# The first layer's gate and up projections as seven half products per pair of output tiles, with the down projection in a stage of its own

## The chip, the cores and the metric

The kernel runs on one core of one Trainium2 chip. The metric is the device time of one execution in microseconds (us), taken as the median of three runs.

## The reference, cut to what matters

The reference is one inference step of a two-layer decoder trunk for 1024 prompt tokens and 64 sample tokens (1088 together), with a model width of 1024. Layer 0 mixes tokens with a short gated convolution, layer 1 with a Conformer convolution. After the mixer, each layer adds a feed-forward part and a gated embedding:

```python
h = h + mix
h = h + swiglu_ffn(rms_norm(h, g_ffn[i]), ffn_w_gu[i], ffn_w_down[i])
gate = jax.nn.sigmoid(rms_norm(h, g_ple[i]) @ ple_w_gate[i])
h = h + gate * (p[i] @ ple_w_proj[i])

def swiglu_ffn(x, w_gu, w_down):
    g, u = jnp.split(x @ w_gu, 2, axis=-1)
    return (jax.nn.silu(g) * u) @ w_down
```

The hidden width of the feed-forward part is 2816, so `x @ w_gu` is 1088 x 1024 by 1024 x 5632, and the down projection is 1088 x 2816 by 2816 x 1024. Everything is float32.

## The kernel before

Activations lie transposed, with 128 channels on the partitions and tokens along the free axis: `h[0]` to `h[7]` are the eight tiles of the residual stream, 128 x 1088 each. A float32 product is made of three matmuls in a faster format: weights and data are each split into a high part and a low part (the rest), and `block` (L259) adds high x high, high x low and low x high. All tokens of layer 0 form the group `GJ`, whose 1088 columns are three matmuls of 288, 512 and 288 columns.

`item` (L274) makes one output tile: for each tile of the contraction a block of 9 matmuls, into one of two PSUM buffers of the pool `ps_j`. Weights come in units of 128 x 1024 (eight blocks). `prep_to` (L201) keeps three units ready: a DMA on SyncE's queue into one of two raw buffers, a ScalarE copy to `whi`, and for `wlo` a GpSimd subtraction `raw - whi`. For later layers, whose units are used twice, `stage` (L231) works ahead during the first layer's feed-forward part: every 6.3 us of a modelled TensorE clock it loads a unit on ScalarE's DMA queue, copies it to the one buffer `shi` on ScalarE, subtracts on GpSimd, and writes the low part to DRAM (`dlo`); later, `wlo` is loaded from there. There are 110 such units.

Instructions are written out by hand in program order, and each engine works through its own in that order. SyncE and ScalarE each issue their DMAs in order, too, and wait before a DMA whose data or buffer isn't ready.

Layer 0 runs as `mixer_a` (L448) and `ffn` (L516), both through `hidden` (L496), which mixes up projections with partial down projections over a few hidden tiles (`MIX_SPLIT`, `FFN_SPLIT`). After an `item` of a down projection VectorE adds it to `h` (`add_h`, L440). In the last part of a down projection, each finished tile of `h` is split at once for the next stage (`norm_split`: ScalarE writes the high part, VectorE the low part), and its squares are added up (`norm_stat`, L377: ScalarE squares, GpSimd or VectorE adds). The sum over channels and its reciprocal root `r` (`rms`, L422) are made while the next stage already multiplies; `r` is applied to the products:

```python
for f in up:    psg = item(y); t = silu(psg * r) * r; psu = item(y); t = psu * t; split t into act
for j in 0..7:  h[j] += item(act tiles of this part)
```

In the code, each hidden tile of the feed-forward part (22 of them) is thus two items of eight blocks.

Of the kernel before, what the change touches and what calls it, by code (L numbers as in the profile page):

```python
# [13 lines left out]
F32 = mybir.dt.float32  # L14
F32R = mybir.dt.float32r
# [45 lines left out]
MIX_SPLIT = [2, 3, 3]  # L61
N_UNITS_0 = 4 * KD + 3 * KF
# [17 lines left out]

GB1 = Group(HALF, 320, [(0, 320)], 0, 512)
# [56 lines left out]
class Net:  # L138
# [3 lines left out]
    def __init__(self, ctx, tc, xT, wall, pT, sa, sb, vecs, yT, sa_p, sa_s, sb_p, sb_s):  # L142
# [11 lines left out]
        self.to_stage = deque(dict.fromkeys(self.order[len(first):]))  # L154
        self.staged, self.staging, self.stage_raw = {}, None, deque()
        self.pst, self.stage_at = None, 0.0
# [9 lines left out]

    def fetch_to(self, n):
        while self.n_raw < min(n, len(self.order)):
            i = self.n_raw % (self.RAW + len(self.spare))
            if i < self.RAW:  # L170
                t = self.pw.tile([P, KD * P], F32, name="wraw", tag="wraw", bufs=self.RAW)
# [7 lines left out]
    def fetch_first(self, piece):  # L179

        for u in range(2):
            if piece == 0:
                self.raw[u] = self.pw.tile([P, KD * P], F32, name="wraw", tag="wraw", bufs=self.RAW)
# [4 lines left out]
    def prep_first(self, piece):  # L188
        nc = self.nc
        for u in range(2):  # L190
            if piece == 0:
                self.hi[u], self.lo[u] = (
                    self.pw.tile([P, KD * P], F32R, name=n, tag=n, bufs=self.RING)
                    for n in ("whi", "wlo"))
# [6 lines left out]
    def prep_to(self, n):  # L201

        nc = self.nc
        while self.n_prep < min(n, len(self.order)):
# [5 lines left out]
            if kind == "w":  # L210
                hi, lo = (
                    self.pw.tile([P, KD * P], F32R, name=n, tag=n, bufs=self.RING)
                    for n in ("whi", "wlo"))
# [17 lines left out]
    def stage(self):  # L231
# [4 lines left out]
        if nc.tensor.at < self.stage_at or self.pst is None:  # L236
            return
        self.stage_at = max(self.stage_at + self.STAGE_EVERY, nc.tensor.at - 2 * self.STAGE_EVERY)
        done, self.staging = self.staging, None
        nc.scalar.wait(nc.tensor)  # L240
        if done is not None:
            u, lo = done
            self.staged[u] = self.pd.tile([P, KD * P], F32, name=f"dlo{u}")
            nc.scalar.dma_start(self.staged[u], lo)
        ready = len(self.stage_raw) == self.STAGE_AHEAD or not self.to_stage
        if ready and self.stage_raw:
            u, raw = self.stage_raw.popleft()
            hi = self.pst.tile([P, KD * P], F32R, name="shi", tag="shi", bufs=1)
# [4 lines left out]
        if self.to_stage:  # L253
            u = self.to_stage.popleft()
            raw = self.pst.tile([P, KD * P], F32, name="sraw", tag="sraw", bufs=self.STAGE_AHEAD + 3)
            nc.scalar.dma_start(raw, self.wall[u])
            self.stage_raw.append((u, raw))


    def block(self, g, ps, blk, x, first, last):  # L260
# [3 lines left out]
        for i, (w, part) in enumerate(((whi, 0), (whi, 1), (wlo, 0))):  # L264
            for c, n in g.chunks:
                self.nc.tensor.matmul(
                    ps[:, g.base + c:g.base + c + n], w, x[:, part, c:c + n],
# [144 lines left out]
    def sum_p(self, g, parts, use):  # L412

        for i, (c, n) in enumerate(g.chunks):
            if g is GJ:
# [6 lines left out]
    def rms(self, g, begin, end):  # L422
# [6 lines left out]
        def two():  # L429
            v = self.tmp(g, "nv")  # L430
# [17 lines left out]
    def mixer_a(self, y):  # L448
# [44 lines left out]

        return self.hidden(g, MIX_SPLIT, up, acts, 0, "g_ffn")

    def hidden(self, g, split, up, acts, layer, gain, bg=None, swap=lambda: None, groups=None):  # L496
        groups = groups or [g]
        out = {q: [] for q in groups}
        for op in hidden_order(split):
# [4 lines left out]
            for j in range(KD):  # L504
                self.add_h(g, j, self.item(g, [acts[k0 + i] for i in range(n)]))
                if b == len(split) - 1:
                    if j == 0:
                        swap()
                    for q in groups:
                        out[q].append(self.norm_split(q, j, self.vec(gain, layer * KD + j)))  # L510
                    self.norm_stat(g, j)
                self.after(bg)
        return [out[q] for q in groups]


    def ffn(self, g, layer, y, bg=None, **kw):  # L516
# [27 lines left out]
        return self.hidden(g, FFN_SPLIT, up, acts, layer, "g_ple", bg, **kw)  # L544
# [335 lines left out]
    def run(self):  # L880
# [20 lines left out]
        for j in range(KD):  # L901
            self.h[j] = ph.tile([P, T], F32, name=f"h{j}")
# [280 lines left out]
```

## Time and profile before

| | |
|---|---|
| median of three runs | 2551.38 us (2550.46 to 2551.61) |
| profiled execution, its own time | 2547.9 us |
| its span, first to last instruction | 2546.1 us |
| mean granted TensorE clock | 0.996 |
| TensorE (PE) busy | 2518.0 us, 99% |
| VectorE (DVE), ScalarE (ACT), GpSimd (POOL) busy | 1068.5, 909.6, 978.0 us |
| DMA | 429.07 MB, mean 169 GB/s |

The times are of one execution each; the profile is of an execution of its own, which took 2547.9 us. "PE" is matmul time, "PEld" are the weight loads, which overlap it. The mixer of layer 0 runs from about 9 to 395 us of the span, its feed-forward part to about 1185 us; the rest of the kernel is the same before and after.

### The profile page before, as it was taken

What the parts mean: (1) busy time and instruction counts of PE and PEld (TensorE: products, weight loads), DVE (VectorE), ACT (ScalarE), POOL (GpSimd) and SP (SyncE); (2) the same over time, 40 slices, a digit from 0 to 9 for tenths busy, and PEclk for the clock granted to TensorE, in tenths of its full rate; (3) what the DMA queues carried; (4) which work ended last, traced back from release to release, by engine and by line L of the source; (5) the groups of instructions that cost most, each with busy time, mean ns of one, the idle gap of its engine ahead of it and who ended that gap; (6) DMA issues with size and microseconds to landing.
All of it is one profiled execution on the core that took longest, in us unless ns stands there. A gap on an engine that the chain in (4) does not pass through costs nothing.

```text
span 2546.1 us, 36304 instructions
## 1 busy us (share of the span) xinstructions
PE 2518.0 (99%) x15062; PEld 2283.9 (90%) x15062; DVE 1068.5 (42%) x1546; ACT 909.6 (36%) x1106; POOL 978.0 (38%) x552
## 2 busy tenths in 40 slices
PE   9999999999999999999999999999999999999997
PEld 8999998999999999998789897888887999999997
DVE  6222234212221212215587676787774622222235
ACT  5111123322332332325555436443435532222235
POOL 3323246756666666653244243333341210000012
PEclk9999999999999999999999999999999999999999
DMA  3111113656565656643565565555556665445445
GB/s 133 56 47 43 43 51 125 225 180 210 202 210 190 207 190 209 212 169 138 181 210 180 167 177 189 189 187 187 190 173 207 208 244 198 166 164 165 163 163 195
DMA packets 143236, 429.07 MB, mean 169 GB/s; under 512 B 33888, under 2 KB 37344, under 8 KB 143072
## 3 DMA queue, kind: packets, MB, share of 16 engines
q1 hardware_dynamic: 110240, 309.17, 36.9%
q10 hardware_dynamic: 32832, 117.59, 13.3%
q8 instruction: 118, 1.93, 0.3%
q14 instruction: 46, 0.38, 0.0%
HBM read 358.94 MB, written 67.76 MB: 168 GB/s over the span
## 4 chain that ended last, share of the span: by engine, by line
PE 96%; DVE 2%; ACT 1%; DMA 0%; issue 0%; DVEq 0%; SPq 0%; ACTq 0%
PE ps L121 96%; DVE t L121 0%; DVE nt L121 0%; DMA wlo<-dlo 0%; DVE acc L121 0%; DVE h L121 0%; DVE hna L121 0%; DVE nv L121 0%; DVE act L121 0%; DMA h<-xT 0%; ACT ua L121 0%; ACT act L121 0%; ACT L121 0%; ACT cact L121 0%; DVE r L121 0%
## 5 line engine op out<-in xcount | busy, mean ns | idle before, releaser
L121 PE MATMUL ps<-hn,whi 128*128 128x288 f32 (+3 forms) x6528 | 1322.8, 325 | 3.5 <-DVE t L121 1.7
L121 PEld LDWEIGHTS ps<-hn,whi 128*128 128x128 f32 x6528 | 1012.8, 189 | 89.7 <-issue 3.0
L121 PE MATMUL ps<-hn,wlo 128*128 128x288 f32 (+3 forms) x3264 | 795.7, 325 | 2.6 <-DMA wlo<-dlo 2.6
L121 PEld LDWEIGHTS ps<-hn,wlo 128*128 128x128 f32 x3264 | 524.9, 189 | 44.8 <-DMA wlo<-dlo 2.8
L121 PE MATMUL ps<-act,whi 128*128 128x288 f32 (+1 forms) x2496 | 511.8, 329 | 1.5 <-DVE act L121 1.4
L121 ACT ACTIVATE whi<-wraw 128x1024 fp32r<-128x1024 f32 (+1 forms) x326 | 339.3, 1043 | 345.3 <-PE ps L121 304.3
L121 PEld LDWEIGHTS ps<-act,whi 128*128 128x128 f32 x2496 | 387.4, 188 | 39.8 <-DVE act L121 2.6
L121 POOL TENSOR_TENSOR t<-t,r 128x1088 f32<-128x1088 f32 (+2 forms) x74 | 136.5, 1844 | 626.8 <-ACT t L121 581.8
L121 POOL TENSOR_TENSOR wlo<-wraw,whi 128x1024 fp32r<-128x1024 f32 (+1 forms) x98 | 240.6, 2457 | 249.7 <-ACT whi L121 233.4
L121 DVE TENSOR_TENSOR h<-ps,h 128x1088 f32<-128x1088 f32 (+2 forms) x216 | 205.5, 952 | 251.0 <-PE ps L121 250.7
L121 PE MATMUL ps<-act,wlo 128*128 128x288 f32 (+1 forms) x1248 | 303.3, 328 | 0.0
L121 POOL TENSOR_TENSOR sraw<-sraw,shi 128x1024 fp32r<-128x1024 f32 x110 | 265.7, 2415 | 79.9 <-issue 61.3
L121 DVE TENSOR_TENSOR t<-ps,r 128x512 f32<-128x512 f32 (+4 forms) x138 | 107.3, 780 | 369.9 <-PE ps L121 369.2
L121 DVE TENSOR_TENSOR t<-ps,t 128x1088 f32<-128x1088 f32 (+2 forms) x89 | 80.8, 908 | 422.5 <-PE ps L121 410.7
L121 POOL TENSOR_TENSOR sqacc<-sqacc,sq 128x512 f32<-128x512 f32 (+4 forms) x76 | 118.0, 1552 | 274.8 <-ACT sq L121 274.5
L121 PEld LDWEIGHTS ps<-act,wlo 128*128 128x128 f32 x1248 | 198.5, 188 | 18.2
L121 ACT ACTIVATE shi<-sraw 128x1024 fp32r<-128x1024 f32 x110 | 115.7, 1052 | 242.8 <-POOL sraw L121 242.0
L121 ACT ACTIVATE t<-t 128x512 f32<-128x512 f32 (+4 forms) x106 | 75.9, 717 | 334.4 <-DVE t L121 334.3
L121 POOL TENSOR_TENSOR prod<-prod 128x512 f32<-128x512 f32 x96 | 124.3, 1302 | 182.3 <-ACT prod L121 182.1
L121 ACT ACTIVATE act<-t 128x1088 fp32r<-128x1088 f32 (+2 forms) x74 | 62.4, 844 | 292.6 <-DVE t L121 292.1
L121 DVE SCALAR_TENSOR_TENSOR acc<-ub,vecs_sb,acc 128x512 f32<-128x512 f32 x184 | 137.5, 748 | 4.0 <-ACT acc L121 4.0
L121 DVE SCALAR_TENSOR_TENSOR acc<-ua,vecs_sb,acc 128x512 f32<-128x512 f32 x184 | 129.2, 750 | 6.3 <-ACT acc L121 4.8
(123 smaller groups left out, 1630.5 us busy)
## 6 DMA issues: line engine op xcount, KB each, us to landing
wraw<-wall SPq DMA_DIRECT2D x322, 512.0 KB, 3.4
wlo<-dlo SPq DMA_DIRECT2D x226, 512.0 KB, 3.4
sraw<-wall ACTq DMA_DIRECT2D x110, 512.0 KB, 4.1
dlo<-sraw ACTq DMA_DIRECT2D x110, 512.0 KB, 2.9
h<-xT SPq DMA_DIRECT2D x8, 544.0 KB, 6.4
pp<-t SPq DMA_DIRECT2D x8, 288.0 KB, 2.4
ub<-pp SPq DMA_DIRECT2D x8, 288.0 KB, 4.7
pp<-t SPq DMA_DIRECT2D x8, 256.0 KB, 2.7
```

The costliest lines, as they stand in the source:

```text
L121: return f(out, *args, **kw)
```

## The change

The gate tile and the up tile of one hidden tile `f` are taken together as the two output halves of a 2 x 2 block product: weights `A11`, `A12` (gate, lower and upper half of the contraction) and `A21`, `A22` (up), tokens in two halves of 544 (`TH`), `B11`, `B12`, `B21`, `B22`. Strassen's scheme in Winograd's form needs seven products of half size in place of eight, with sums of weights (`S1` to `S4`) and of tokens (`T1` to `T4`). One `product` has four contraction tiles, three matmul passes and two pieces of 272 columns (`GS`): 24 matmuls. Seven go into one hidden tile.

The token side (`operands`) is made in the last part of the mixer's down projection, after each second tile of `h` (order `MIX_J`, parts now 2, 2 and 4 hidden tiles); its 28 cells take the place of the old `hn` tiles and of six tiles of `h`, which is written to DRAM (`hd`). The weight side (`pair_fetch`, `pair_sums`, `pair_cell`) is made one hidden tile ahead. The hidden tiles' results go to DRAM (`ad`). Then `h` is loaded again, and `ffn0_down` makes the down projection in parts of 3, 4, 4, 4, 4 and 3 hidden tiles, each loaded and split anew. `stage` now works in half units (220) from 50 us on, every 4.4 us of the modelled clock, with a pause between the mixer's last part and the up stage; what is left is staged in `swap`, after the first item of the last part. The layer's arithmetic is otherwise the same.

```diff
-MIX_SPLIT = [2, 3, 3]
+MIX_SPLIT = [2, 2, 4]
+MIX_J = [0, 4, 1, 5, 2, 6, 3, 7]
+DOWN_0 = [3, 4, 4, 4, 4, 3]
+GS = Group(0, T, [(0, TH // 2), (TH // 2, TH // 2)], HALF - TH // 2, 1024)
...
+    def stage(self, flush=False):
+        nc = self.nc
+        if self.stage_slots is None or not flush and nc.tensor.at < self.stage_at:
             return
         self.stage_at = max(self.stage_at + self.STAGE_EVERY, nc.tensor.at - 2 * self.STAGE_EVERY)
         done, self.staging = self.staging, None
+        ahead = len(self.stage_slots) - 3
         if done is not None:
+            nc.scalar.dma_start(self.staged[u][:, i * WH:(i + 1) * WH], lo)
+        ready = len(self.stage_raw) == ahead or flush or not self.to_stage
         if ready and self.stage_raw:
             u, raw = self.stage_raw.popleft()
+            hi = self.stage_slots[0]("shi", F32R)
             nc.scalar.activation(hi, raw, AF.Copy)
             nc.gpsimd.tensor_tensor(raw.bitcast(F32R), raw, hi.bitcast(F32), ALU.subtract)
             self.staging = u, raw
+        if self.to_stage and not flush:
+            nc.scalar.dma_start(raw, self.wall[u][:, i * WH:(i + 1) * WH])
+    def stage_with(self, slots):
+        while self.stage_raw or self.staging:
+            self.stage(True)
+        self.stage_slots, self.stage_at = slots, self.nc.tensor.at
...
+    ORDER = "A11", "S2", "S3", "S1", "S4", "A12", "A22"
+    ORDER_0 = "A11", "A12", "S2", "S3", "S1", "S4", "A22"
+    def pair_fetch(self, i):
+        raw = [self.wtile("wraw", k) for k in range(2)]
+        ...
+        for k, t in enumerate(raw):
+            self.nc.sync.dma_start(t, self.wall[N_MIX + 2 * i + k])
+    def pair_sums(self, i):
+        for d, a, b, op in ("S1", "A21", "A22", ALU.add), ("S2", "S1", "A11", ALU.subtract), (
+                "S4", "A12", "S2", ALU.subtract), ("S3", "A11", "A21", ALU.subtract):
+            nc.vector.tensor_tensor(p[d], p[a], p[b], op)
+    def pair_cell(self, i, name):
+        nc.scalar.activation(w[:, 0], src, AF.Copy)
+        (nc.gpsimd if name[0] == "A" else nc.vector).tensor_tensor(
+            w[:, 1], src, w[:, 0].bitcast(F32), ALU.subtract)
+    def product(self, ps, w, xs):
+        for k, x in enumerate(xs):
+            for i, (h, part) in enumerate(((0, 0), (0, 1), (1, 0))):
+                for c, n in GS.chunks:
+                    self.nc.tensor.matmul(...)
+            self.stage()
...
+    def mixer_end(self, i, ps):
+        g, j = GJ, MIX_J[i]
+        if i == 0:
+            self.at_end[0]()
+        if i == KD - 1:
+            self.at_end[1]()
+        self.add_h(g, j, ps)
+        self.nc.sync.dma_start(self.hd[j], self.h[j])
+        if i % 2:
+            self.operands(j - KH)
+        self.norm_stat(g, j, self.nc.vector)
+        if i == KD - 3:
+            self.pair_fetch(0)
+    def operands(self, k):
+        def put(name, src, scale=None):
+            x = self.right[name, k] = pool.tile([P, 2, TH], F32R, name="y7", tag=tag, bufs=1)
+            self.split(x, src, scale)
+        put("B11", ha[:, lo], ga)
+        nc.scalar.activation(ya, ha, AF.Copy, scale=ga)
+        put("B21", hb[:, lo], gb)
+        nc.scalar.activation(yb, hb, AF.Copy, scale=gb)
+        nc.vector.tensor_tensor(ya[:, lo], ya[:, up], ya[:, lo], ALU.subtract)
+        nc.vector.tensor_tensor(ya[:, up], yb[:, up], ya[:, up], ALU.subtract)
+        put("T1", ya[:, lo])
+        nc.vector.tensor_tensor(yb[:, up], yb[:, up], ya[:, lo], ALU.subtract)
+        put("T2", yb[:, up])
+        put("B22", hb[:, up], gb)
+        put("T3", ya[:, up])
+        nc.vector.tensor_tensor(yb[:, lo], yb[:, lo], yb[:, up], ALU.subtract)
+        put("T4", yb[:, lo])
...
+    def ffn0_up(self):
+        for f in range(KF):
+            if f == 0:
+                rms[0]()
+                self.pair_fetch(1)
+            def go(a, b):
+                ps = self.psum(GS)
+                self.product(ps, self.cell.pop((f, a)), [self.right[b, k] for k in range(KH)])
+                return ps[:, GS.base:GS.base + TH]
+            nc.scalar.activation(t[:, lo], go("A11", "B11"), AF.Copy)
+            if f == 0:
+                nc.scalar.activation(t[:, up], t[:, lo], AF.Copy)
+                add(t[:, lo], go("A12", "B21"), t[:, lo])
+            next_weights(0)
+            add(t[:, up], go("S2", "T2"), t[:, lo] if f else t[:, up])
+            if f == 0:
+                rms[1]()
+            next_weights(1)
+            add(s[:, lo], go("S3", "T3"), t[:, up])
+            next_weights(2)
+            q = go("S1", "T1")
+            add(t[:, up], q, t[:, up])
+            add(s[:, up], q, s[:, lo])
+            next_weights(3)
+            add(t[:, up], go("S4", "B22"), t[:, up])
+            next_weights(4)
+            if f:
+                add(t[:, lo], go("A12", "B21"), t[:, lo])
+            nc.vector.tensor_tensor(t, t, r, ALU.mult)
+            nc.scalar.activation(t, t, AF.Silu)
+            nc.vector.tensor_tensor(s[:, up], s[:, up], r[:, up], ALU.mult)
+            add(s[:, lo], go("A22", "T4"), s[:, lo])
+            nc.vector.tensor_tensor(s[:, lo], s[:, lo], r[:, lo], ALU.mult)
+            nc.vector.tensor_tensor(t, t, s, ALU.mult)
+            nc.sync.dma_start(self.ad[f], t)
+    def ffn0_down(self, places, swap):
+        def load():
+            nc.sync.dma_start(t, self.ad[f])
+            nc.scalar.activation(high, t, AF.Copy)
+            nc.vector.tensor_tensor(low, t, high.bitcast(F32), ALU.subtract)
+        for _ in range(DOWN_0[0]):
+            load()
+        for b, n in enumerate(DOWN_0):
+            last = b == len(DOWN_0) - 1
+            for j in range(KD):
+                self.add_h(g, j, self.item(g, acts[at:at + n]))
+                if not last:
+                    if j < DOWN_0[b + 1]:
+                        load()
+                    continue
+                if j == 0:
+                    swap()
+                for q in out:
+                    out[q].append(self.norm_split(q, j, self.vec("g_ple", j)))
+                self.norm_stat(g, j)
...
+        self.pps = pool("ps_s", c_ps, space=PSUM, bufs=4)
+        self.ffn0_up()
+        self.stage_with(None)
+        self.pps = pool("ps_d", c_ps, space=PSUM, bufs=2)
+        for j in 3, 7, 4, 0, 1, 5, 2, 6:
+            nc.sync.dma_start(self.h[j], self.hd[j])
         def swap():
+            for _ in range(len(self.to_stage)):
+                self.stage_at = 0.0
+                self.stage()
+            self.stage_with(None)
+        ya, yb = self.ffn0_down(places, swap)
...
-    STAGE_EVERY = 6.3
+    STAGE_EVERY = 4.4
+    STAGE_FROM = 50.0
```

`next_weights(m)` makes the next hidden tile's `pair_sums` at m = 0 and its seven `pair_cell` at m = 1 to 4, then fetches the pair after it (for f = 0, two steps later).

## Rows read from the trace of the kernel before

**Rows 1.** The page: engines busy; below, shares of the chain of waits.

```profile
PE 2518.0 (99%) x15062; PEld 2283.9 (90%) x15062; DVE 1068.5 (42%) x1546; ACT 909.6 (36%) x1106; POOL 978.0 (38%) x552
...
PE 96%; DVE 2%; ACT 1%; DMA 0%; issue 0%; DVEq 0%; SPq 0%; ACTq 0%
```

**Rows 2.** Busy time by stretch (us, instructions), then granted clock, DMA share, GB/s.

```profile
100.00:400.00 300.00, 299.61 (x1801) 272.10 (x1801) 85.14 (x80) 62.35 (x64) 105.54 (x54) 1.00 0.16 47
400.00:420.00 20.00, 19.91 (x121) 17.86 (x120) 9.40 (x7) 5.07 (x5) 12.48 (x5) 1.00 0.43 150
420.00:800.00 380.00, 378.28 (x2287) 345.01 (x2286) 86.50 (x67) 114.76 (x112) 240.79 (x100) 1.00 0.58 198
800.00:1200.00 400.00, 399.52 (x2391) 362.94 (x2390) 98.30 (x86) 132.60 (x136) 241.45 (x100) 1.00 0.55 189
```

**Rows 3.** Timeline of the mixer: start, duration; first and last of 11 blocks.

```profile
300.16 0.95 PEld L121 LDWEIGHTS ps<-hn,whi 128*128 128x128 f32 x6
...
315.07 0.95 PEld L121 LDWEIGHTS ps<-hn,whi 128*128 128x128 f32 x6
```

**Rows 4.** Timeline, 288-column matmuls: first and last of 9 such pieces.

```profile
2451.95 0.70 PE L121 MATMUL ps<-hn,whi 128*128 128x288 f32 x4
...
2458.34 0.69 PE L121 MATMUL ps<-hn,whi 128*128 128x288 f32 x4
```

**Rows 5.** Timeline, 256-column matmuls: first and last of 15 such pieces.

```profile
2509.91 0.40 PE L121 MATMUL ps<-hn,whi 128*128 128x256 f32 x2
...
2514.90 0.40 PE L121 MATMUL ps<-hn,whi 128*128 128x256 f32 x2
```

**Rows 6.** Groups by shape: count, busy, mean ns of one, idle before, releasers.

```profile
L121 ACT ACTIVATE whi<-wraw 128x1024 fp32r<-128x1024 f32 x322 | 336.9, 1048 | 345.3 <-PE ps L121 304.3 <-issue 34.1 <-POOL sqacc L121 3.6
...
L121 POOL TENSOR_TENSOR wlo<-wraw,whi 128x1024 fp32r<-128x1024 f32 x96 | 236.6, 2465 | 239.2 <-ACT whi L121 222.9 <-issue 16.1
...
L121 ACT ACTIVATE shi<-sraw 128x1024 fp32r<-128x1024 f32 x110 | 115.7, 1052 | 242.8 <-POOL sraw L121 242.0 <-ACT whi L121 0.9
L121 DVE TENSOR_TENSOR h<-ps,h 128x1088 f32<-128x1088 f32 x88 | 113.6, 1291 | 181.1 <-PE ps L121 181.1
...
L121 DVE SCALAR_TENSOR_TENSOR hn<-h,vecs_sb,hn 128x576 fp32r<-128x576 f32 x31 | 25.3, 819 | 16.6 <-ACT hn L121 16.6
L121 ACT ACTIVATE hn<-h,vecs_sb 128x576 fp32r<-128x576 f32 x32 | 24.5, 771 | 33.8 <-DVE h L121 33.6
...
L121 ACT ACTIVATE sq<-h 128x1088 f32<-128x1088 f32 x21 | 22.8, 1097 | 0.0
...
L121 POOL TENSOR_TENSOR prod<-prod,c 128x512 f32<-128x512 f32 x14 | 18.1, 1293 | 0.1
...
L121 DVE TENSOR_TENSOR act<-t,act 128x512 fp32r<-128x512 f32 x22 | 16.0, 728 | 15.4 <-ACT act L121 15.4
...
L121 DVE SCALAR_TENSOR_TENSOR hn<-h,vecs_sb,hn 128x512 fp32r<-128x512 f32 x16 | 12.0, 752 | 12.7 <-ACT hn L121 12.7
L121 ACT ACTIVATE hn<-h,vecs_sb 128x512 fp32r<-128x512 f32 x16 | 11.6, 724 | 25.3 <-DVE h L121 25.3
```

**Rows 7.** Timeline: GpSimd and VectorE side by side.

```profile
415.66 2.56 POOL L121 TENSOR_TENSOR sraw<-sraw,shi 128x1024 fp32r<-128x1024 f32 x1 [1.99 <-ACT shi L121]
...
415.99 3.37 DVE L121 SCALAR_TENSOR_TENSOR nt<-nt,nv 128x1088 f32<-128x1088 f32 x1
```

**Rows 8.** Busy time by stretch: around a TensorE wait.

```profile
1438.00:1442.00 4.00, 1.74 (x14) 1.50 (x12) 3.56 (x7) 3.09 (x5) 2.91 (x3) 1.00 0.80 175
1442.00:1446.00 4.00, 3.69 (x19) 3.69 (x20) 2.35 (x4) 1.06 (x1) 0.50 (x1) 0.67 1.09 374
```

**Rows 9.** DMA issues: KB each, median us to landing.

```profile
wraw<-wall SPq DMA_DIRECT2D x322, 512.0 KB, 3.4
...
h<-xT SPq DMA_DIRECT2D x8, 544.0 KB, 6.4
```

**Rows 10.** Busy time by stretch: transfers at their densest.

```profile
2500.00:2510.00 10.00, 10.00 (x73) 10.00 (x72) 4.39 (x10) 5.12 (x9) 2.55 (x3) 1.00 1.01 384
```

More of the change, by code (lines that the diff above doesn't have):

```diff
@@ L153, in __init__ @@
         self.n_raw = self.n_prep = self.blk = 0
-        self.to_stage = deque(dict.fromkeys(self.order[len(first):]))
+        self.limit = N_MIX
+        self.n_conv = 0
+        self.pairs, self.cell = {}, {}
+        self.to_stage = deque((u, i) for u in dict.fromkeys(self.order[len(first):]) for i in range(2))
         self.staged, self.staging, self.stage_raw = {}, None, deque()
-        self.pst, self.stage_at = None, 0.0
+        self.stage_slots, self.stage_at = None, 0.0
         self.bg = deque()
@@ L191, in prep_first @@
             if piece == 0:
-                self.hi[u], self.lo[u] = (
-                    self.pw.tile([P, KD * P], F32R, name=n, tag=n, bufs=self.RING)
-                    for n in ("whi", "wlo"))
+                self.hi[u], self.lo[u] = self.wpair()
             c = self.FIRST[piece]
@@ L210, in prep_to @@
             if kind == "w":
-                hi, lo = (
-                    self.pw.tile([P, KD * P], F32R, name=n, tag=n, bufs=self.RING)
-                    for n in ("whi", "wlo"))
+                hi, lo = self.wpair()
             else:
@@ L503, in hidden @@
             _, b, k0, n = op
-            for j in range(KD):
-                self.add_h(g, j, self.item(g, [acts[k0 + i] for i in range(n)]))
+            for i, j in enumerate(js):
+                ps = self.item(g, [acts[k0 + i] for i in range(n)])
+                if last and b == len(split) - 1:
+                    last(i, ps)
+                    continue
+                self.add_h(g, j, ps)
                 if b == len(split) - 1:
[L507 to L510, printed above, removed]
+                    out.append(self.norm_split(g, j, self.vec(gain, layer * KD + j)))
@@ new lines, in run @@
+        self.pps = pool("ps_s", c_ps, space=PSUM, bufs=4)
+        self.PSW = GS.width
+        self.stage_with(self.stage_tiles(pool("stage_u", c_st), 5))
+        self.ffn0_up()
+        self.stage_with(None)
+        c_st.close()
+        self.n_conv += 2
+        c_x.close()
+        c_ps.close()
+        c_ps = ExitStack()
+        self.pps = pool("ps_d", c_ps, space=PSUM, bufs=2)
+        self.PSW = 0
+        py, py2 = self.cells["T2", 0][0], self.cells["B11", 0][0]
+        for j in range(KD):
+            self.h[j] = ph.tile([P, T], F32, name=f"h{j}", tag=f"h{j}")
```

198 lines of the change are left out of this document (151 added, 47 removed).

## The prediction

> **What bounds the kernel now.** I read the page first: TensorE is busy 99% of the span, and the chain of waits lies on it for 96% [rows 1]. So only two things count: how long TensorE's own work takes, and how long it is made to wait. The windows over the part that is rewritten show how little it waits today: between 100 and 1200 us it is idle for 0.39 + 0.09 + 1.72 + 0.48 = 2.7 us, at full clock, while VectorE is busy for about a quarter of the time [rows 2]. A change that shortens TensorE's work therefore gives its full saving, less every wait that it brings. The groups by shape give prices for the other engines [rows 6].
>
> **What the seven products save.** Before, a hidden tile is 16 blocks of 9 matmuls. Ten blocks start 315.07 - 300.16 = 14.91 us apart [rows 3], so one takes 1.491 us and a hidden tile 23.86. Matmuls of 272 columns aren't in the trace. Those of 288 start every (2458.34 - 2451.95) / 48 = 133.1 ns [rows 4], those of 256 every (2514.90 - 2509.91) / 42 = 118.8 ns [rows 5]; 272 lies halfway, 126.0 ns. A product is 24 of them, 3.02 us, seven are 21.2 us. The saving is 2.70 us a hidden tile, **59.4 us** over 22, about an eighth less a little for the shorter pieces. The down projection keeps its blocks, so it costs the same. The 2.7 us of old waits go, too, since each stood at an edge that no longer exists. Everything else is about new waits, and I find three.
>
> **First seam: mixer to up stage.** Each item of the mixer's last part is now four blocks, 5.96 us; a pair of items gives TensorE 11.9 us. Per pair VectorE adds twice to `h` (1.29 each), adds squares twice (like the add, 1.29) and makes the operands: seven low parts and four subtractions of 544 columns. Between the 512- and 576-column rows a scaled low part is 0.79 and a scaled high part on ScalarE 0.75; a plain subtraction is about 0.73, an unscaled copy 0.65 by ScalarE's rate of 1.10 for 1088 [rows 6]. VectorE's own operand work is 3 x 0.79 + 8 x 0.73 = 8.2 us. But each low part waits for the high part that ScalarE makes just before, and the copies `ya` and `yb` (1.2 each) stand in ScalarE's queue: walking the lists in order, operands take 11.4 us. The pair is 1.29 + 1.10 (square) + 1.29 for the first tile, 1.29 + 11.4 + 0.4 + 1.29 for the second: 18.1 us on VectorE against 11.9 on TensorE.
>
> With two PSUM buffers an item can't start before the add of the item two before it. Counted from the start of the last part, VectorE is through with pair 0 at 11.9 + 14.4 = 26.3, so item 4 starts at 27.6 in place of 23.9 (wait 3.7); with pair 1 at 44.4, so item 6 starts at 45.7 in place of 39.5 (wait 6.2). Item 7 ends at 57.6. VectorE ends pair 2 at 62.5, tile 6 at 66.2, and only then come, queued ahead of the last add, four weight sums and four weight low parts: 8 x 0.7 = 5.6, with about 3 more where GpSimd's `A` cells get in the way. The add ends at 76, the last tile's `B11` at 77.8. TensorE has meanwhile done three of the first product's four contraction tiles (2.3 us), so it waited 17.9. The sums for `r` are in its queue behind the third product and need the other operands (9.9), the last squares (1.7) and the split of the sum (2.4): 91.6, against 85 where TensorE could have begun, 6.8 more. VectorE then still owes the reciprocal root (4 operations), the next tile's sums and cells, and PSUM releases: some 11 more until it has caught up. Together 3.7 + 6.2 + 17.9 + 6.8 + 11 = 45.6. Independent instructions overlap slightly, so I take **44**. Lower bound: VectorE's own work alone, 13.4 a pair, is 4.5 behind after three pairs, plus 5.6 and 2.1 for add and `B11`: 12. Upper bound, with 7% longer instructions: 55.
>
> **Second seam: up to down stage.** The last product's result still passes three VectorE operations (0.72 + 0.73 + 1.29 = 2.7 us) before `ad[21]` can be written. That write is in SyncE's queue, and behind it stand, in this order, the eight reloads of `h`, the three `ad` reads and the first weight unit: SyncE waits, so none of them starts earlier. 544 KB are 557,000 bytes, 1.45 us at the 384 GB/s that full DMA engines moved [rows 10]. Twelve such transfers and one of 512 KB (1.37) are 18.8 us; a lone 512 KB transfer lands 3.4 us after issue, so 2.0 are fixed, and 6.4 for `h` from the input shows what queueing adds [rows 9]. The weights are there at 2.7 + 2.0 + 18.8 = 23.5. ScalarE's `whi` takes 1.05, GpSimd's `wlo` 2.47 [rows 6]; TensorE does two passes of a block (1.0) meanwhile. The wait is **26**; I take 27 with the semaphore hops. Lower bound 15, if the reloads (8 x 1.45) were not in the way; upper 36, at a lower rate.
>
> **Third wait: what is left to stage.** 110 units are 220 halves. On the modelled clock (0.0025 us a matmul plus 0.00042 a column) the staging window in the mixer, 50 to 319 us, gives 62 halves at 4.4 us, the up stage (432 us) 99, the down stage up to `swap` (216 us) 50: 211. Nine are left for `swap`, and three are loaded but not done. All twelve are issued on ScalarE ahead of the first split of `h`. There is one `shi` buffer, so each copy waits for GpSimd's subtraction, as it does today, 242 us in all [rows 6]: 0.6 + 1.29 + hops = 1.95 us a step, 23 us. ScalarE begins some 3 us before item 0 ends and is free 20 us after it; two splits and the add of item 1 end at 23.7. VectorE waits in its queue for those splits, so item 3 has no PSUM buffer, while TensorE had work (items 1 and 2) for 9: a wait of **15**. Bounds 0 (ScalarE ran far ahead) and 17.
>
> **Clock.** [...] Three long waits: **4**, from 0 to 7.
>
> **Cover that I cost at nothing.** In the up stage VectorE has per hidden tile 7 results from PSUM (0.72 each), 8 weight operations (0.7), 2 of 544 (0.73) and 2 of 1088 (1.29): 14.7 of 21.2 us; ScalarE about 9, GpSimd 9.6. Four PSUM buffers let VectorE lag by three products, 9 us. Pair loads are 1 MB each 21 us. In the down stage a load adds 1.29 to VectorE in an item of at least 4.5. The mixer's earlier staging falls behind the operations that release PSUM.
>
> **The sum.** -59.4 - 2.7 + 44 + 27 + 15 + 4 = +28 us. Against the profiled execution's 2547.9 that is 2576; the median of the runs shown is 3.5 above that execution, so I forecast a median of **2579 us**, 1.1% slower.
>
> **Rivals.**
> *Faster: the operands are ready in time.* Place: the chain of ScalarE and VectorE in the mixer's last part. If it is hidden under the items and the weight cells are done before item 7, the first seam falls to between 12 and 0, and the time to 2547 to 2535. For it: both engines are mostly idle today [rows 2]. Against it: they work in turns. It decides where the seam costs under 16 (no change), and below 11 a gain can be told; about 0.2% (5 us) is what this measurement can tell.
> *Slower still: VectorE and GpSimd bar each other in the loop.* An operation on two SBUF operands took 3.37 us while GpSimd subtracted, and ended 1.14 us after it [rows 7]; undisturbed 1088 columns take 1.29. In the loop VectorE has 12 such operations (9.6 us) and GpSimd 9.6. If they alternate, 19.2 and the 5 us from PSUM overlap enough for 21.2. If GpSimd holds on for two operations in a row, a walk through the lists gives 23.5 us a tile: 22 x 2.3 = 50 more, 2629. [...]
> *Each wait costs half.* Half of 44 + 27 + 15 is 43 less: 2536. No single row asks for it; it stands for my walks through the queues being too strict.
>
> **How the numbers follow.** Forecast (slower by 5 to 60 us) 0.66; operands in time, or all waits halved, faster, 0.22; near no change 0.05; loop bound 0.07. So faster 0.22, same 0.05, slower 0.73. With all lower bounds the sum is -35 (2516), with all upper ones +53 (2604); a range of 2525 to 2612 leaves about one in ten on each side. The forecast's own range is 2557 to 2612.
>
> **What would show it.** Right: gaps of TensorE before items 4 and 6 and the first product, with VectorE busy without pause; about 25 us of idle TensorE before the first down matmul with the reloads of `h` landing in it; ScalarE and GpSimd in alternation at `swap`; 21.2 us a tile in between. Wrong: a tile of 23 us or more, a seam below 15, or TensorE busy through `swap`.

## The result, and the profile after

The changed kernel took **2595.37 us** (median of 4 runs, 2593.68 to 2597.56), against 2550.92 us of the kernel before on the same chip (4 runs, 2546.71 to 2551.61): a ratio of 1.0178, 95% interval 1.0161 to 1.0196. It is 44 us slower, where 28 were forecast on the profiled execution. That execution took 2593.68 us with a span of 2591.9.

First the page: busy times by engine, and the group of the new products.

```profile
PE 2476.4 (96%) x15590; PEld 2283.1 (88%) x15590; DVE 1403.2 (54%) x1947; ACT 1001.4 (39%) x1377; POOL 952.3 (37%) x655
...
L128 PE MATMUL ps<-y,w 128*128 128x272 f32 x3696 | 472.3, 290 | 11.6 <-ACT w L128 3.4
```

TensorE works 2518.0 - 2476.4 = 41.6 us less than before [rows 1], and stands idle 2591.9 - 2476.4 = 115.5 us, where it was 2546.1 - 2518.0 = 28.1: 87.4 more. The two make up the whole 45.8 us by which the spans differ. So there are two questions: where the idle time is, and why TensorE saved only 41.6.

The waits of TensorE, all of the span (total, times, longest):

```profile
PE ps L128 <- DVE h L128: 47.1, 6, 27.2
PE ps L128 <- ACT whi L128: 28.5, 2, 26.2
```

Two single waits of 26.2 and 27.2 us are more than half of the 87.4. The windows of 25 us show the places (window, its length, TensorE busy with its matmuls, granted clock, DMA share, GB/s):

```profile
200.00:225.00 25.00, 21.81 (x132) 1.00 0.48 148
225.00:250.00 25.00, 24.51 (x138) 0.93 0.47 157
...
375.00:400.00 25.00, 15.65 (x87) 0.80 0.11 45
400.00:425.00 25.00, 18.21 (x92) 0.84 0.29 110
425.00:450.00 25.00, 17.89 (x95) 0.68 0.29 100
...
700.00:725.00 25.00, 25.00 (x200) 1.00 0.53 180
...
900.00:925.00 25.00, 6.15 (x49) 0.67 0.67 252
925.00:950.00 25.00, 15.42 (x81) 0.78 0.65 237
950.00:975.00 25.00, 23.03 (x128) 0.93 0.58 195
...
1175.00:1200.00 25.00, 5.45 (x34) 0.70 0.62 206
1200.00:1225.00 25.00, 17.30 (x91) 0.75 0.20 71
```

Between 500 and 900 us TensorE is busy without a gap at full clock: 200 or 201 matmuls of 272 columns in 25 us, some 125 ns each, and 21.05 us a hidden tile. All of the loss lies in four places, and in each of them the clock falls too. Idle time by place, with what the kernel before had in the same stretch taken off: mixer (0 to 350) 5.8 us, first seam (350 to 500) 24.9, second (900 to 975) 30.4, third (975 to 1225) 26.8; together 87.9, and 0.5 less than before in the rest.

**First seam.** The timeline of the changed kernel (start, duration, engine; in brackets the idle time before it and what ended it). The mixer's last part begins at 352.40.

```profile
369.53 0.63 ACT L128 ACTIVATE shi<-sraw 128x512 fp32r<-128x512 f32 x1 [1.88 <-POOL sraw L128]
...
371.61 0.33 ACTq L128 DMA_DIRECT2D dlo<-sraw  x1
...
373.00 0.73 ACT L128 ACTIVATE y<-h,vecs_sb 128x544 fp32r<-128x544 f32 x1
...
386.91 2.15 PE L128 MATMUL ps<-act,whi 128*128 128x288 f32 x6 [9.35 <-DVE h L128]
...
388.45 1.19 ACT L128 ACTIVATE ya<-h,vecs_sb 128x1088 f32<-128x1088 f32 x1
...
402.72 1.43 PE L128 MATMUL ps<-act,whi 128*128 128x288 f32 x6 [2.22 <-DVE h L128]
...
420.04 0.81 PE L128 MATMUL ps<-y,w 128*128 128x272 f32 x4 [3.45 <-ACT w L128]
...
428.45 0.82 PE L128 MATMUL ps<-y,w 128*128 128x272 f32 x2 [2.94 <-ACT y L128]
...
441.41 0.61 PE L128 MATMUL ps<-sh,ones_r 128*128 128x288 f32 x1 [2.64 <-ACT sh L128]
```

ScalarE issues the last write of leftover staging at 371.61, and only then makes the first operand, at 373.00. So item 4 waits 9.35 us; item 6 then waits 2.22, and the first product four times, 3.45, 1.12, 2.94 and 0.81 us (two of them shown): 8.3 in all.

**Second seam.** The same view, for SyncE's queue (SPq), ScalarE and TensorE. The last product ends at 906.15.

```profile
909.97 0.32 SPq L693 DMA_DIRECT2D ad<-t  x1
910.34 7.14 SPq L1206 DMA_DIRECT2D h<-hd  x8
919.76 1.27 SPq L709 DMA_DIRECT2D ta<-ad  x3
921.13 13.96 SPq L193 DMA_DIRECT2D wraw<-wall  x3
...
931.23 1.06 ACT L128 ACTIVATE whi<-wraw 128x1024 fp32r<-128x1024 f32 x1
932.34 2.18 PE L128 MATMUL ps<-act,whi 128*128 128x288 f32 x6 [26.19 <-ACT whi L128]
...
951.94 1.26 PE L128 MATMUL ps<-act,whi 128*128 128x288 f32 x6 [3.91 <-DVE h L128]
```

The order on SyncE's queue is the predicted one: `ad`, eight `h`, three `ta`, then weights. The `whi` copy ends the wait.

**Third wait.** The first line is the first of the twelve copies at `swap`, 0.5 us after TensorE began item 1 (1171.41). The lines below it are one step of staging; such steps repeat from 1179 to 1204 us.

```profile
1171.94 0.64 ACT L128 ACTIVATE shi<-sraw 128x512 fp32r<-128x512 f32 x1 [3.70 <-POOL sraw L128]
...
1199.29 0.63 ACT L128 ACTIVATE shi<-sraw 128x512 fp32r<-128x512 f32 x1 [1.86 <-POOL sraw L128]
1200.05 1.26 POOL L128 TENSOR_TENSOR sraw<-sraw,shi 128x512 fp32r<-128x512 f32 x1 [1.23 <-ACT shi L128]
1201.35 0.33 ACTq L128 DMA_DIRECT2D dlo<-sraw  x1
1201.77 0.63 ACT L128 ACTIVATE shi<-sraw 128x512 fp32r<-128x512 f32 x1 [1.85 <-POOL sraw L128]
...
1204.20 0.72 ACT L128 ACTIVATE hna<-h,vecs_sb 128x512 fp32r<-128x512 f32 x1 [1.80 <-POOL sraw L128]
...
1207.69 1.51 PE L128 MATMUL ps<-act,whi 128*128 128x288 f32 x4 [27.24 <-DVE h L128]
```

From copy to copy a step takes 1201.77 - 1199.29 = 2.48 us: the copy (0.63), GpSimd's subtraction (1.26), then the write of `dlo`, whose issue on ScalarE's queue takes 0.33 and waits for GpSimd, and the hops between them. The next copy would have to wait for GpSimd in any case, as there is one `shi` buffer. The split `hna` at 1204.20 needs nothing of the staging, and yet stands idle for 1.80 us until GpSimd is done, behind the last write.

**Why only 41.6 us of work were saved.** At 125.3 ns each (399 in 50 us of the undisturbed loop) the 3696 matmuls of the products would be busy 463.1 us; they were 472.3, 9.2 more. The matmuls on `act`, whose number did not change, were busy 367.6 + 300.3 + 217.3 + 164.1 = 1049.3 us before and 372.6 + 303.8 + 219.5 + 165.8 = 1061.7 after, 12.4 more. These 21.6 us lie where the windows show a granted clock under 1: six matmuls of 288 and 512 columns that take 1.16 us inside the items take 2.15 after the wait of 9.35.

### The profile page after: what moved, and what is told of

The parts are those of the page before. It is cut to its first block, busy times and chain, and to the rows that moved or that the text cites. A ratio compares the mean times of both kernels' runs of the same rounds, so it can differ in the third digit from the quotient of the medians.

```text
span 2591.9 us, 39114 instructions
## 1 busy us (share of the span) xinstructions
PE 2476.4 (96%) x15590; PEld 2283.1 (88%) x15590; DVE 1403.2 (54%) x1947; ACT 1001.4 (39%) x1377; POOL 952.3 (37%) x655
## 3 DMA queue, kind: packets, MB, share of 16 engines
q8 instruction: 123, 2.02, 0.3%
## 4 chain that ended last, share of the span: by engine, by line
PE 50%; DVE 2%; ACT 1%; DMA 1%; POOL 0%; issue 0%; ACTq 0%; DVEq 0%; POOLq 0%; SPq 0%
PE ps L128 50%; DMA dlo<-sraw 0%; POOL sraw L128 0%; DVE t L128 0%; DMA wlo<-dlo 0%; DVE acc L128 0%; DVE h L128 0%; ACT ua L128 0%; DVE hna L128 0%; DVE nt L128 0%; ACT cact L128 0%; ACT shi L128 0%; ACTq L128 0%; DMA sraw<-wall 0%; DVE nv L128 0%
## 5 line engine op out<-in xcount | busy, mean ns | idle before, releaser
L128 PE MATMUL ps<-hn,whi 128*128 128x288 f32 (+3 forms) x4416 | 915.1, 323 | 3.2 <-ACT whi L128 2.3
L128 PEld LDWEIGHTS ps<-hn,whi 128*128 128x128 f32 x4416 | 692.7, 189 | 58.5 <-ACT whi L128 2.5
L128 PE MATMUL ps<-hn,wlo 128*128 128x288 f32 (+3 forms) x2208 | 562.8, 323 | 2.6 <-DMA wlo<-dlo 2.6
L128 PE MATMUL ps<-y,w 128*128 128x272 f32 x3696 | 472.3, 290 | 11.6 <-ACT w L128 3.4
L128 PEld LDWEIGHTS ps<-y,w 128*128 128x128 f32 x3696 | 470.9, 190 | 13.1 <-ACT w L128 3.8
L128 POOL TENSOR_TENSOR sraw<-sraw,shi 128x512 fp32r<-128x512 f32 x220 | 318.6, 1448 | 359.8 <-issue 131.7
L128 PEld LDWEIGHTS ps<-hn,wlo 128*128 128x128 f32 x2208 | 364.8, 189 | 29.6 <-DMA wlo<-dlo 2.9
L128 ACT ACTIVATE shi<-sraw 128x512 fp32r<-128x512 f32 x220 | 137.6, 625 | 300.6 <-POOL sraw L128 285.6
L128 DVE TENSOR_TENSOR t<-ps,t 128x544 f32<-128x544 f32 (+3 forms) x155 | 115.4, 746 | 255.4 <-PE ps L128 247.8
L128 POOL TENSOR_TENSOR wlo<-wraw,whi 128x1024 fp32r<-128x1024 f32 (+1 forms) x54 | 136.1, 2524 | 138.2 <-ACT whi L128 132.3
```

The lines of the kernel that those rows point to most:

```text
L128: return f(out, *args, **kw)
```

## The experiments

Times of e1 to e5, e7 and e8 are of one run each (no experiment has the number 6), beside 2549.5 us (e1 to e4) or 2548.9 (e5 to e9) of the kernel before; differences under some 3 us are not read from them. e9 to e13 have four or more runs each.

### The pace of the staging, both ways

`STAGE_EVERY` is 4.4 in the changed kernel. e1 sets 4.0, e2 sets 4.8.

```diff
-    STAGE_EVERY = 4.4
+    STAGE_EVERY = 4.0      (e1; in e2 4.8)
```

e1: 

> Staging paced at 4.0 us in place of 4.4, so that by the count of the modelled clock nothing is left for the place after the first item of the last down part. Theory (the wait there is the burst of staging steps queued on ScalarE ahead of the first split): the 27.2 us wait before item 3 of the last part goes, 2595 becomes about 2567. Rival (the wait belongs to the splits, the PSUM buffers or the reloaded h): it stays, 2590 to 2600. Second rival (the steps cost as much wherever they stand): the wait goes, but the mixer and the other stages grow by as much.

e2: 

> Staging paced at 4.8 us, so that 27 half units are left in place of 9. Theory (the wait is a burst of steps of 2.49 us each): 18 steps more, 45 us, about 2640, with a wait of about 72 us at that place. Rival (the wait belongs to something else): within 5 us of 2595.

e1 took 2572.41 us, 23.0 less; e2 2633.35, 38.0 more. The waits of TensorE from 950 us on (to 1260 in e1, to 1300 in e2) are, in e1:

```profile
PE ps L128 <- DVE h L128: 3.6, 1, 3.6
```

and in e2:

```profile
PE ps L128 <- DVE h L128: 71.9, 3, 68.0
```

The wait at `swap` goes to nothing with a faster pace (the 3.6 us of e1 lie at 957, in the second seam) and grows to 68.0 us with a slower one. Less staging left over is the whole of it, and the cause of the third wait is shown. The wait and the lower clock behind it were worth more than 23 us: from the last product to the first matmul of the gated embedding e1 takes 296.7 us (911.91 to 1208.62), the changed kernel 326.3 (906.15 to 1232.45). But the last product ends 5.8 us later. The mixer, which now stages more, ends 2.2 of them later, and TensorE waits there 4.5 us for ScalarE's `t`, which it did not before; the other 3.6 are not explained.

### The leftover staging at the mixer's end

e5 is e1 with the loaded units finished at the start of the mixer's last up projection, one hidden tile before the last part, instead of at its first item.

```diff
         def up(f):
+            if f == KD - 1:
+                self.stage_with(None)
```

> The pace of 4.0 us, and staging stops before the mixer's last up tile, so that its leftover steps (361 to 371.6 us on ScalarE) no longer stand ahead of the first operands. Theory (the seam is a chain on ScalarE and VectorE that begins late): operands begin 5 to 6 us earlier and the whole seam with them, 2572 becomes about 2566; the wait before item 4 falls from 9 to about 4. Rival (the seam's length is set at its end, by the weight sums and the last tile): the wait before item 4 shrinks and a later one grows, total within 2 us of 2572.

It took 2563.58 us, 8.8 less than e1. Item 4 of the last part, from TensorE's timeline of e5:

```profile
394.60 2.15 PE L128 MATMUL ps<-act,whi 128*128 128x288 f32 x6 [3.52 <-DVE h L128]
```

The wait is 3.5 us, where it is 9.35 in the changed kernel and 8.8 in e1. The prediction's walk through the queues gave 3.7 for it, without the staging.

### Who sets the pace of the first seam

e7 makes the same operands in another order: ScalarE's high parts first, and each of VectorE's low parts only when its high part is long done. e4 gives the adding of squares in the last part to GpSimd, which takes 1.29 us twice per pair from VectorE.

```diff
e7   high("B11") ya yb high("B21") low("B11") sub high("T1") sub high("T3")
     sub high("T2") sub high("T4") high("B22") low("B21") low("T1") ... low("B22")
e4
-        self.norm_stat(g, j, self.nc.vector)
+        self.norm_stat(g, j)
```

e7: 

> The same operand operations in another order: ScalarE's copies and high parts are issued ahead, the four subtractions in a row, the low parts last, so that VectorE seldom waits for ScalarE. Theory (VectorE and ScalarE work in turns, which costs some 2.5 us in each of four pairs): 7 to 10 us less, about 2587. Rival (VectorE's own 13.4 us a pair against TensorE's 11.9 and the weight sums make the seam): less than 3 us of change.

e4: 

> The sums of squares of the mixer's last part are added by GpSimd in place of VectorE. Theory (VectorE's queue is what the seam waits for): 7 additions of 1.29 us and the waits for four squares leave VectorE's queue, the seam is 5 to 14 us shorter, total 2581 to 2590. Rival (GpSimd's additions on two operands in SBUF hold VectorE up): VectorE's operand operations grow to 2 us and more in places, total 2593 to 2605.

e7 took 2587.49 us, 7.9 less: item 4 waits 7.66 us, item 6 no more, and the sums 0.5 in place of 2.6. So part of the seam is VectorE waiting for ScalarE, as forecast, and part of it can be had by order alone. e4 took 2596.23, no change. Its timeline shows why:

```profile
384.02 2.51 POOL L128 TENSOR_TENSOR sqacc<-sqacc,sq 128x1088 f32<-128x1088 f32 x1 [12.73 <-ACT sq L128]
...
386.77 5.66 DVE L128 SCALAR_TENSOR_TENSOR y<-h,vecs_sb,y 128x544 fp32r<-128x544 f32 x2 [0.67 <-ACT y L128]
...
388.83 3.03 POOL L128 TENSOR_TENSOR sqacc<-sqacc,sq 128x1088 f32<-128x1088 f32 x1
```

Two low parts, 1.69 us together in the changed kernel at 390.35, take 5.66 while GpSimd first makes a `wlo` (386.49 to 388.88) and then adds. So here VectorE pays beside GpSimd's work what it was spared, and more: 5.66 - 1.69 = 3.97 us for 2 x 1.29. This is what the rival expected of the loop, seen in an experiment, and yet it does not stop the loop, where TensorE of the changed kernel is busy 25.00 of 25 us.

### The order on SyncE's queue

e3 puts the reads of `ad` and two weight units ahead of the eight reloads of `h`. e8 goes further: those reads, the weights and two of the `h` are issued before the end of the up stage, `act` is split ahead of the leftover staging, and the other six `h` are loaded one by one between the first items.

```diff
e3
         for _ in range(DOWN_0[0]):
             load()
+        self.fetch_to(self.n_raw + 2)
+        reload()
...
-        for j in 3, 7, 4, 0, 1, 5, 2, 6:
-            nc.sync.dma_start(self.h[j], self.hd[j])
+        def reload():
+            for j in 3, 7, 4, 0, 1, 5, 2, 6:
+                nc.sync.dma_start(self.h[j], self.hd[j])
...
e8
+            if f == KF - 1:
+                self.begin_down()     # weights, three reads of ad, h[3], h[7]; ahead of the S4 product
...
+            if f == KF - 1:
+                self.begin_acts()     # ScalarE and VectorE split them; ahead of the write of ad[21]
```

e3: 

> At the start of the down stage the three loads of hidden tiles and the first two weight units stand ahead of the eight reloads of h in SyncE's queue. Theory (the 26.2 us wait is SyncE's order and the bytes ahead of the first weights): 8 x 1.45 = 11.6 us less, wait 14 to 15, total about 2584. Rival (the write of the last hidden tile and the conversions on ScalarE and GpSimd set the start): within 3 us of 2595, wait still over 23.

e8: 

> The first three loads of hidden tiles, two weight units and two tiles of h are issued four products before the up stage ends, ahead of the write of the last hidden tile; their splits stand ahead of the leftover staging steps; the other tiles of h are reloaded one by one during the first down part. Theory (the 26.2 us are SyncE's order plus the bytes ahead, and what the reordering of the reloads alone won came back because the third weight unit still stood behind them): the wait falls to between 5 and 11 us and none comes back, total 2575 to 2580. Rival (transfers are the limit whatever their order): a wait of 8 us or more comes back in the first down part, total above 2585.

e3 took 2592.67 us, 2.7 less, where 11 were expected. Its timeline:

```profile
923.20 2.18 PE L128 MATMUL ps<-act,whi 128*128 128x288 f32 x6 [15.63 <-ACT whi L128]
...
925.62 15.04 SPq L193 DMA_DIRECT2D wraw<-wall  x3
...
936.78 1.06 ACT L128 ACTIVATE whi<-wraw 128x1024 fp32r<-128x1024 f32 x1 [12.30 <-DMA wraw<-wall]
...
940.71 0.90 SPq L709 DMA_DIRECT2D ta<-ad  x2
```

and from its waits of TensorE, 460 to 950 us:

```profile
PE ps L128 <- DVE h L128: 9.2, 1, 9.2
```

The first wait fell to 15.6 us, near the 14 to 15 worked out. But the third weight unit, issued at 925.62, still landed behind the eight reloads, and its copy began only at 936.78, some 11 us later (the median from issue to landing is 3.9 in the changed kernel). The next unit on SyncE's queue waits for a raw buffer until GpSimd has made the `wlo` (940.30), and the read of the next part's first hidden tile (`ta`) stands behind it, at 940.71. Its low part stands on VectorE ahead of the add to `h` that TensorE then waits for, 9.2 us. So most of the gain came back by another path. e8 took 2583.81, 11.6 less. TensorE's timeline of its seam:

```profile
912.29 1.27 PE L128 MATMUL ps<-act,whi 128*128 128x288 f32 x3 [2.73 <-ACT whi L128]
916.77 1.27 PE L128 MATMUL ps<-act,whi 128*128 128x288 f32 x3 [3.21 <-DVE act L128]
...
938.67 2.18 PE L128 MATMUL ps<-act,whi 128*128 128x288 f32 x6 [6.17 <-DVE h L128]
```

With a fourth wait of 1.1 us at 950.90, 13.2 us of waiting are left of 26.2 + 0.3 + 3.9 = 30.4, 17.2 less. From the last product to the first matmul of the gated embedding e8 takes 310.2 us (909.56 to 1219.74), 16.1 less than the changed kernel's 326.3. That the time fell by 11.6 only lies outside this stretch: the last product ends 3.4 us later, and what follows the gated embedding's start takes 2.8 us longer (to the end of the spans, 2581.9 and 2591.9). The edit leaves both parts alone; whether this is scatter, one run can't tell.

### All four together

e9 joins e1, e5, e7 and e8.

> All four together: pace 4.0, early stop, operands in the new order, loads ahead. Theory (three separate waits that add up): 2595 - 23 (measured for the pace) - 6 - 8 - 17 = about 2541, some 0.3 to 0.4% faster than the kernel before. Rival (the waits share a cause, or the products save less than 59 us): 2550 or more.

It took **2537.79 us** (5 runs, 2535.70 to 2541.02), a ratio to the kernel before of 0.996, 95% interval 0.9947 to 0.9974: 0.4% faster than the kernel before, and faster than the changed one. The four gains, 23.0 + 8.8 + 7.9 + 11.6 = 51.3, make 2544; it is 6 us better. From its page:

```profile
PE 2475.0 (98%) x15590; PEld 2282.6 (90%) x15590; DVE 1404.9 (55%) x1947; ACT 1000.2 (39%) x1377; POOL 956.6 (38%) x655
```

TensorE is busy as long as in the changed kernel (2476.4), so the lower clock still costs it some 20 us; what the edits took away is 56.5 us of idle time (115.5 to 2534.0 - 2475.0 = 59.0).

### The clock, apart from the waits

Would keeping TensorE at work through the waits give those 20 us back? e10 to e13 put matmuls of a constant matrix, 128 columns each and read by nobody, into the waits: e10 three groups into the first seam, e11 375 ahead of the down stage and 390 ahead of the item that waits at `swap`, e12 four groups into e9, e13 again the changed kernel with fewer.

```diff
+    def fill(self, ps, n):
+        for _ in range(n):
+            self.nc.tensor.matmul(ps[:, :P], self.ones_r, self.ones_r, start=True, stop=True)
...
         ps = self.psum(g)
+        if fill:
+            self.fill(ps, fill)
```

e10: 

> The changed kernel with matmuls of a constant matrix put into three waits of the first seam: 45 ahead of the first product (about 3.0 us at 65 ns each, that is 118.8 ns at 256 columns less 128 at the slope to 288), 70 ahead of its fourth contraction tile (4.6 us), 60 ahead of the sums for r (3.9 us). Their results are read by nobody. In the changed kernel the matmuls of 272 columns are busy 472.3 us, against 463.1 at 125.3 ns each: 9.2 us at the lower clock, nearly all in this seam. Theory one (VectorE and ScalarE set the seam's pace, so the slow matmuls hide under waits that would be there anyway): the granted clock stays near 1.0 from 416 to 448 us, the busy time of the 272-column matmuls falls to about 464 us, and yet the kernel is only 1 to 3 us faster than the changed one, by what follows the last wait. Theory two (the slow matmuls are on the path): 8 to 9 us faster, 2587. Theory three (the constant matmuls are themselves late work ahead of the products): slower by 2 to 5 us.

e11: 

> The changed kernel with 375 constant matmuls (24.4 us) ahead of the first item of the down stage, where TensorE waits 26.2 us, and 390 (25.4 us) ahead of the item that waits 27.2 us at the hand-over to the gated embedding. Their results are read by nobody. After the second wait the first blocks ran at half clock (10 matmuls in 3.39 us where 10 take 1.6: 1.8 us), after the third 2.18 + 2.02 for twelve that take 2.3 and 1.11 for three that take 0.66: 2.3 us. Theory one: the second seam gives nothing, since the next wait there (3.9 us, for an add to h) only gets longer; the third gives 2 us: 2593. Theory two (both are on the path): 4 us, 2591. Theory three (the constant matmuls come too late or too many): slower by up to 3 us.

e12: 

> The version that joins the early hand-over of staging, the pace of 4.0, the other order of the operands and the earlier loads (2537.8 us), with 40, 70 and 45 constant matmuls in the first seam and 30 ahead of the first item of the down stage. It has 9.7 us of lower clock in its 272-column matmuls and 8.6 in those of the down stage and the mixer. Theory one (hidden under waits): 0 to 3 us faster, 2535 to 2538. Theory two (on the path): 8 to 10 us faster, 2529.

e13: 

> The changed kernel with constant matmuls in three waits, sized by the 112 ns that one of 128 columns took in the last runs (42.09 us for 375): 26 (2.9 us) ahead of the sums for r, 225 (25.2 us) ahead of the first item of the down stage, 235 (26.4 us) ahead of the item that waits at the hand-over. They end about when the old waits ended. What ran at the lower clock behind these waits in the changed kernel: the sums and the next 32 matmuls, 2.7 us over their time at full clock; ten matmuls at the second seam, 1.8; fifteen at the third, 2.3. Theory one (the slow matmuls hide under the waits that come next): 0 to 2.3 us faster than the changed kernel, 2593 to 2595, and the next wait of the second seam, 3.9 us, grows to 5 or 6. Theory two (they are on the path): 5 to 7 us faster, 2588 to 2590. Of the whole 20 us that TensorE lost to the clock, the 10 us or so before the sums are not touched by this.

Three times it was slower: e10 2604.28 us, e11 2618.14, and e12, against e9, 2550.24. The estimate of 65 ns was wrong. From e11's timeline:

```profile
906.66 42.09 PE L128 MATMUL ps<-ones_r 128*128 128x128 f32 x375 [0.82 <-DVE s L128]
948.59 1.22 PE L128 MATMUL ps<-act,whi 128*128 128x288 f32 x6
...
1190.46 43.66 PE L128 MATMUL st<-ones_r 128*128 128x128 f32 x390
```

One takes 42.09 / 375 = 112 ns at full clock (1.00 from 908 to 948 us), so both groups outlast the wait that they were to fill, by some 16 us each. In e10 and e12 they also took a PSUM buffer that the first product then had to wait for. But e11 shows two things: the clock is not lost (1.00 from 948 to 952 us, and six matmuls take 1.22 us right behind the group), and the time rose by 22.8 us and not by 32, as lost clock and a later wait of 3.9 us went.

e13 is sized by 112 ns. Its median is 2599.83 us, with more scatter than the others (2595.07 to 2612.18, the kernel before beside it 2545.97 to 2555.09), ratio 1.0214, interval 1.0186 to 1.0242; so it is not faster. Its timeline:

```profile
952.77 2.18 PE L128 MATMUL ps<-act,whi 128*128 128x288 f32 x6 [3.08 <-DVE h L128]
...
1182.48 26.35 PE L128 MATMUL st<-ones_r 128*128 128x128 f32 x235
1209.03 1.26 PE L128 MATMUL ps<-act,whi 128*128 128x288 f32 x6 [0.21 <-DVE h L128]
```

At the second seam the group ends 1.56 us early; the first six matmuls behind it take 1.27 us (933.26), near the 1.16 inside the items, but after one more wait, 1.19 us for `wlo`, the next six take 1.97. And what was won is lost again: the next wait for `h` ends at 952.77, in the changed kernel at 951.94. The third seam's blocks do run at full clock at once (1.00 from 1200 to 1225 us); by the time of the whole this can't be told. So the slow stretches are real, but at least at the second seam they stand in for waiting that would come anyway. For the first seam this was not shown: e10 did not keep the clock there (0.50 from 420 to 432 us), and e13 touched only its end.

## Why the prediction was right

The sign holds, and the time lies in the forecast's own range: three new waits cost more than the products save, each at the place that was named and on the engines and queues that were named. The size was forecast too small, 28 us for 45.8, and single terms miss in both directions. Term by term, forecast and measured (idle time net of before; lower clock by what matmuls took over their time at full clock: in the windows from 925 to 975 us 209 matmuls were busy 38.45 us, which at 153 in 25 us take 34.15; from 225 to 250 us it is 24.51 for 22.55; at the third seam 2.3; what is left of 9.2 + 12.4, some 13, is the first seam's):

| step | forecast | measured |
|---|---|---|
| products | -59.4 | 22 x (23.86 - 21.05) = -61.8 |
| old waits | -2.7 | in the lines below |
| first seam | +44 | 24.9 idle, and about 13 of lower clock |
| second seam | +27 | 30.4 idle, and about 4 |
| third wait | +15 | 26.8 idle, and about 2 |
| mixer, earlier staging | 0 | 5.8 idle, and about 2 |
| clock | +4 | about 21, in the lines above |
| rest of the kernel | 0 | -1.3, the remainder |
| sum | +28 | +45.8 |

**Products.** 272 columns halfway between 256 and 288 gave 126.0 ns; 125.3 was measured, 21.05 us a tile for 21.2.

**First seam.** The total of about 38 us is 6 less than forecast, but its shape was wrong, and that the totals come so near is luck: 13 of the 38 are lower clock, which the forecast had in another term, at 4 for all three waits. The walk started the first operands at once; they had to wait for leftover staging on ScalarE, which the prediction costed at nothing there (e5), so item 4 waited 9.35 for 3.7. VectorE then took less than walked: its pair, from the add at 389.15 to the next at 404.96, is 15.8 us for the forecast 18.1, so item 6 waited 2.2 for 6.2, the first product 8.3 for 17.9 and the sums for `r` 3.4 for 6.8 (the walk's own 91.6 against 85 gives 6.6). The difference is a head start of ScalarE: it made `B11`'s high part (387.81) and `ya` (388.45) while VectorE still added squares and `h`; the walk began both after the second add. The operands then took from 390.35 to 399.81, 9.5 us for 11.4. One sign did not come: VectorE was to be busy without pause, and was busy for 40.9 of the 50 us from 400 to 450.

**Second seam.** 26 us were worked out and 26.2 measured, by the same chain; that it is so near is in part luck. The weights' first copy began 25.1 us after the last product (931.23) where the walk had 23.5, and the 1.5 us that the walk had for `wlo` were 0.27, since TensorE's two passes meanwhile ran at the lower clock (0.50 from 932 to 936 us) and took 2.18 us for 1.0. What came after it was not in the sum: the 3.9 us for the next add. That add (950.60) stands on VectorE behind the low part of the next part's first hidden tile (949.39), whose read SyncE issued at 943.63 only, behind weight units that wait for a raw buffer; in e3 the same chain is 9.2 us.

**Third wait.** This is the term that was mis-sized most, 15 for 26.8. The step is 2.48 us and not 1.95: the issue of the write, 0.33, was not in the sum, and "hops" did not cover it. Over twelve steps that is 6.4 us. The start of 3 us that ScalarE was to have ahead of item 0's end did not come, since the first of the twelve copies is 0.5 us behind it (1171.94): 3.5 us more. And 2.5 us went on steps that waited longer, one of them 3.61 us for a write to land (1178.98): from 1171.94 to 1204.20 are 32.3 us, where twelve steps of 2.48 are 29.8.

**Mixer.** Its earlier staging was costed at nothing, as falling behind the operations that release PSUM. It does not quite: at 225 us TensorE waits 3.7 us for an add to `h`. The add stands on VectorE behind a low part of `act`, whose high part ScalarE began at 221.80, behind two staging copies (218.10 and 220.56), though `t` was there at 217.3.

**Clock.** No run shows the 4 us for three long waits; in its place the runs showed about 21 us of matmul time over that at full clock, some 13 of them at the first seam, where the clock was low behind shorter waits as well (0.68 from 425 to 450 us, with waits of 2.94 and 2.64). It is not a term of its own, though, but partly a part of the waits (e13).

**Rivals.** VectorE and GpSimd do not bar each other enough to stop the loop: TensorE is busy 25.00 of 25 us there. Side by side they do take longer (e4: two low parts on VectorE 5.66 us for 1.69, an addition on GpSimd, at 388.83, 3.03 for the 2.51 at 384.02). That the operands are in time is refuted by the waits of the first seam. They are not in time in e9 either: there the first seam still costs 14.3 us of idle time net of before (16.5 of the 150 us from 350 to 500), where this rival allowed 12 at most. That e9's 2537.8 falls between this rival's 2535 and 2547 comes by another road, from all three edges. Nor was each wait half of the forecast: only the first seam's idle time, 24.9 for 44, is near that.

## What to carry to other kernels

A saving on the engine that bounds is kept only if the stages that the change cuts apart are joined again: price each edge by what is queued ahead of the first operation that the bound engine needs, on every queue, DMA queues and leftover background work included. Here four edits of order and pace, with no work taken away, turned 1.8% slower into 0.4% faster. When a background task is made finer, count its steps to the end and price the step with the DMA that it issues, for whatever is left at the hand-over is paid in full.

## What the runs showed of the hardware

- A matmul of 128 columns took 112 ns (e11, x375), hardly less than the 118.8 of one of 256 [rows 5], where the slope from 256 to 288 columns carried on gave 65.
- At full clock matmuls of 272 columns came every 125.3 ns.
- After short waits the granted clock was low: 0.50 from 404 to 406 us of the changed kernel, behind the wait of 2.22 at 402.72, where the second six matmuls took 2.02 us for the 1.16 inside the items. Six took 2.18 after a wait of 3.08 (e13, 952.77) and 2.15 after one of 3.52 (e5, 394.60). Behind constant matmuls in place of the wait it was 1.00 (e11, 948 to 952 us: 1.22 us for the first six).
- A DMA issued on ScalarE's queue that waited for GpSimd held ScalarE's next activation, though that needed nothing of it: 1.80 us of idle time before `hna` at 1204.20. With the 0.33 us of its issue a step of staging took 2.48 us for 0.63 + 1.26 of work.
- A matmul of 512 columns on float32 operands took 592 ns (`s` with `ones`), one on the split parts 395 (`act` with `whi`), both in the kernel before.
